# Feed-forward output products on the two 64-row halves of the array, in four phases of paired blocks

## The chip, the cores and the metric

The kernel runs on one core of a Trainium2 chip. The metric is the device time of one execution in microseconds. Three runs of the kernel before took 1286.21, 1286.5 and 1287.46 us (median 1286.5). A measurement of this kernel tells about 0.2% from no change.

In the profile, PE is the TensorE matrix engine and PEld its weight loads, DVE the vector engine, ACT the scalar engine, POOL the GpSimd engine, and SPq the queue that starts most transfers.

## What is computed

One inference step of a two-layer decoder trunk, for 512 prompt tokens and 8 x 8 sample tokens: layer 0 is a gated recurrent block, layer 1 sliding-window attention, and each is followed by a SwiGLU feed-forward block. All sizes are float32. The change touches the feed-forward block only:

```python
def swiglu(h, w_in, w_out):
    gate, up = jnp.split(h @ w_in, 2, axis=-1)
    return (jax.nn.silu(gate) * up) @ w_out
...
h = modulate(rms_norm(x, norm_g[l, 1]), sh2, sc2)
x = x + g2[:, None, :] * swiglu(h, ffn_w_in[l], ffn_w_out[l])
```

with D_MODEL = 1024 and D_FF = 2816, so `w_out` has 22 x 8 tiles of 128 x 128. The gain g2 (and the shifts and scales) come from modulation products, `silu(c) @ ada_w`, which the kernel spreads over its whole length.

## The kernel before

**Layout.** The 576 tokens are split into two halves h = 0, 1 of HC = 288 columns (256 prompt tokens and 32 sample tokens); features lie on the 128 partitions. The stream `x[h]` stays in SBUF as 8 chunks of 128 features.

**Products.** float32 products are made of single-pass ones (type fp32r): each operand is split into a rounded high part and the rest, and hi*hi + hi*lo + lo*hi are summed in one PSUM bank. So one 128 x 128 weight tile against 288 columns is three TensorE instructions (`product`), each of which loads its own weights. In the profile's names `wh` are split weights, `h`, `sl`, `ta`, `tb`, `td` split activations and working tiles, `mm` PSUM banks. There are 6 such banks (`ps()`), and 2 more for the modulation products (`ada`).

**Weights.** A weight unit is loaded into a `raw` buffer by a transfer, then converted: ACT copies the rounded high part into one `wh` slot, DVE subtracts it to make the low part in another (`convert`). There are 10 slots of 1024 columns (2 * NHI). A unit of feed-forward output weights holds all n middle tiles of a group for one output chunk m, n x 128 columns: 768 in groups of 6, 512 in the last group of 4. It is used for both token halves and then dropped (`drop`), which frees its slots. `todo` lists the conversions in order, and `pump` starts them as slots come free.

**The feed-forward block.** `ffn(l, ...)` goes through the 22 middle tiles in GROUPS = (6, 6, 6, 4). For each group, the input stage makes the group's middle tiles (silu(gate) * up), in seven products each by a scheme that saves one in eight (`seven`, operands "11", "22", "S1" to "S4", "12"); POOL, ACT and DVE prepare the operands, and `whole` splits each finished middle tile into two `sl` tiles, `mid[h][f]`. Then the output stage, `out(k, m, h)`, adds for each output chunk m and token half h the product of the group's n middle tiles into one bank: 3 n instructions, a *block*. `residual` (DVE, with a small sum on POOL) adds the gated block to the stream. A stage has 16 blocks, in the order (m = 0, h = 0), (0, 1), (1, 0), (1, 1), ...; in the last group h = 1 runs LEAD = 4 chunks behind h = 0, so that the norm of h = 0 can begin early. In layer 1's last group `final_chunk` transposes each finished chunk for the output. There are two layers of four groups, so eight output stages of 16 blocks.

**Order of the work.** Every instruction is recorded with its estimated cost and the operations it depends on (`Recorder.add`); `schedule` then simulates the engines and writes one fixed order for each of them, and TensorE's instructions may be interleaved one by one. `together()` records several instructions as one piece that isn't split: so far the batches of modulation products, which use the array as four strips of 32 columns, and the paired score products of the attention, which use 64 rows each. A cost table in `Engine.record` holds the estimates; `mode` names the array's form, and the simulation adds 100 ns where it changes.

Of the kernel before, what the change touches and what calls it, by code (L numbers as in the profile page):

```python
# [13 lines left out]
F32R = mybir.dt.float32r  # L14
# [5 lines left out]
P = 128  # L20
D = 1024
KC = D // P
# [5 lines left out]
HC = 288  # L28
# [100 lines left out]
class Recorder:  # L129
# [9 lines left out]
        self.batch = None  # L139

    @contextmanager
    def together(self):

        self.batch = []
        yield
        b, self.batch = self.batch, None

        def emit():
            for x in b:
                x[1]()  # L150

        self.add(b[0][0], emit, sum(x[2] for x in b), [y for x in b for y in x[3]], [y for x in b for y in x[4]], mode=self.mode)

    def tile(self, pool, kind, cap, reserve, shape, dt, name):
        sh = self.shadow[kind in ("mm", "ada")].tile(shape, dt, tag=name, bufs=1, name="shadow_" + name)
# [223 lines left out]
class Engine:  # L379
# [8 lines left out]
    def record(self, name, args, kw):  # L388
        eng, obj = self.eng, self.obj
        outs, ins, vals = [], [], list(args) + list(kw.values())  # L390
        isap = lambda v: hasattr(v, "ap") and hasattr(v, "tensor")
        first = kw["out"] if "out" in kw else args[0]
        outs.append(first)
        if isap(kw.get("accum_out")):
            outs.append(kw["accum_out"])
        ins = [v for v in vals if isap(v) and not any(v is o for o in outs)]
        f = max([_free(x) for x in outs + ins])
        scal = len([x for x in ins if x is not kw.get("accum_out") and _free(x) == 1 and len(x.ap) <= 2 and f > 1])
        ps_ = any(_is_psum(x) for x in ins)
        func, lat = None, 0  # L400

        reads = [x for x in (list(args) if "out" in kw else list(args[1:])) + [v for n, v in kw.items() if n not in ("out", "accum_out")] if isap(x)]
        wide = [x for x in reads if not _is_psum(x) and not str(x.space).endswith("DRAM") and (_free(x) > 1 or f == 1)]
        port = eng == "POOL" and name != "dma_start" and bool(wide) or eng == "DVE" and not ps_ and (len(wide) > 1 or name == "tensor_scalar" and f > 1)
        port = (2 if eng == "POOL" and f <= 40 else 1) if port else 0
        mode = 0
        if name == "matmul":
            if kw.get("start") is not True:
                ins.append(first)
            n = _free(first)  # L410
            dt = args[2].dtype
            cost = max(n + 32, 264) / 2.4 if dt == F32R else max(214.0 if first.ap[0][1] > 32 else 134.0, n * 4 / 2.4)
            if dt == F32 and 64 in (first.ap[0][1], args[1].ap[0][1]) and n >= P:

                mode = 1 if args[1].ap[0][1] == 64 else 2
                cost = n * 2 / 2.4 + 20
            if first.ap[0][1] == 32 and args[1].ap[0][1] == P and n >= P:
                cost = n / 2.4 + 30 if dt == F32 else n / 9.6 + 15
                mode = 3
        elif name == "transpose":  # L420
            cost = 107.0
        elif name == "dma_start":
            src = args[1]
            n = max(_free(first) * first.ap[0][1], _free(src) * src.ap[0][1])
            cost, lat = (460.0 if eng == "SP" else 1020.0), n * 4 / 335.0 + 5
        elif eng == "ACT":
            cost = (52 if ps_ else 94) + 0.8333 * f + (0, 90, 187)[min(scal, 2)] + (96 if isap(kw.get("accum_out")) else 0)
            func = str(args[2]).split(".")[-1] if name == "activation" else "Copy"
        elif eng == "DVE":
            if name == "reciprocal":  # L430
                cost = 62 + 6.28 * f
            elif name == "memset":
                cost = 20 + 0.5 * f
            elif name == "tensor_tensor_scan":
                cost = 70 + 2.1 * f
            else:
                cost = 67 + 1.0417 * f + (61 if scal and name == "scalar_tensor_tensor" else 0)
        else:
            if name == "tensor_tensor":
                cost = 150 + (165 if ALU.pow in vals else 2.4) * f  # L440
            elif name == "memset":
                cost = 35 + 0.83 * f
            elif name == "tensor_scalar":
                cost = 260 + 3.33 * f if scal else 95 + 1.05 * f
            else:
                cost = 120 + 3.3 * min(f, 32) + max(f - 32, 0) * 1.1
        self.rec.add(eng, lambda: getattr(obj, name)(*map(real, args), **{k: real(v) for k, v in kw.items()}), cost, outs, ins, func, lat, port, mode)  # L447


class Slots:  # L450
# [6 lines left out]
    def __call__(self, dt=None):  # L457
        self.live += 1
        self.n += 1
        self.peak = max(self.peak, self.live)  # L460
        return Slot(self, self.rec.tile(self.pool, self.kind, self.bufs, self.reserve, [P, self.w], dt or self.dt, f"{self.kind}{self.n}"))


class Slot:
# [9 lines left out]
def trunk_kernel(ctx, tc, a):  # L474
    nc = tc.nc
    rec = Recorder(a["shadow"])
# [6 lines left out]
    def const(shape, name, dt=F32):  # L483
        return cp.tile(shape, dt, tag=name, name=name)
# [3 lines left out]
    def ps(pool=pmm, tag="mm"):  # L488
        cnt[0] += 1
        return rec.tile(pool, tag, NMM if tag == "mm" else (8 - NMM), RMM if tag == "mm" else 1, [P, 512], F32, f"{tag}{cnt[0]}")  # L490
# [4 lines left out]
    x = [const([P, KC, HC], f"x{h}") for h in range(2)]  # L495
# [26 lines left out]
    nsp4 = const([P, KC], "nsp4")  # L522
    snk = const([P, 52], "snk")
    hgb = const([P, 16], "hgb")

    make_identity(nc, ident)
    nc.gpsimd.memset(ones, 1.0)
# [402 lines left out]
    class Unit:  # L930
        def __init__(self, kc, srcs):
            self.kc, self.srcs, self.raw, self.hi, self.lo = kc, srcs, None, None, None
            self.left = 2
# [14 lines left out]
    def convert():  # L948
        u = units[nconv[0]]
        if u.raw is None:  # L950
            load_more()
        n = u.kc * P
        u.hi, u.lo = whs(), whs()
        with early(EW):
            S.copy(u.hi.r[:, 0:n], u.raw.f[:, 0:n])
            V.tensor_tensor(u.lo.r[:, 0:n], u.raw.f[:, 0:n], u.hi.f[:, 0:n], ALU.subtract)
        u.raw.done()
        nconv[0] += 1
        nhi[0] += 1

    def drop(u):
        u.left -= 1
        if u.left == 0:
            u.hi.done()
            u.lo.done()
            nhi[0] -= 1

    def unit_cols(w, c0, k0=0, kc=KC):
# [200 lines left out]
    def ffn(l, g, after):  # L1169
# [80 lines left out]
        def queue():  # L1250
            for k, bs in enumerate(blocks):
                for i in range(max(PLAIN, sum(GROUPS[:k])), sum(GROUPS[: k + 1])):
                    st = steps(i)
                    if i == PLAIN:
                        nxt = steps(i + 1)
                        for s_, names in ((st, ("11", "12")), (nxt, ("11", "12")), (st, ("22", "S1", "S2", "S3", "S4")), (nxt, ("22", "S1", "S2", "S3", "S4"))):
                            for n in names:
                                todo.append((1, s_[n]))
                    elif i > PLAIN + 1:
                        for n in ("11", "22", "S1", "S2", "12", "S3", "S4"):  # L1260
                            todo.append((1, st[n]))
                for _ in outs[k][1]:
                    todo.append((2, convert))

        def pump(want=lambda: True):
            while todo and (whs.live + todo[0][0] <= 2 * NHI):
                todo.popleft()[1]()
            assert want()
            load_more()
# [66 lines left out]
            split(m[0].r[:, 0:HC], m[1].r[:, 0:HC], t.f[:, 0:HC])  # L1336
            t.done()

        def out(k, m, h):
            f0, us = outs[k]  # L1340
            n, u = GROUPS[k], us[m]
            pump(lambda: u.hi is not None)
            o = ps()
            product(o[:, 0:HC], u, [(mid[h][f][0].r[:, 0:HC], mid[h][f][1].r[:, 0:HC]) for f in range(f0, f0 + n)])
            last = k == len(GROUPS) - 1
            residual(h, o, m, g, last)
            if last and l == 1:
                final_chunk(h, m)
            drop(u)
            pump()  # L1350
            if m == KC - 1:
                for f in range(f0, f0 + n):
                    for s_ in mid[h][f]:
                        s_.done()
                if last:
                    after(h)

        def emit():
            if l == 1:
# [3 lines left out]
            for k in range(len(GROUPS)):  # L1363
# [23 lines left out]
                            for s_ in pq:  # L1387
                                s_.done()
                lead = LEAD if k == len(GROUPS) - 1 else 0
                for j in range(KC + lead):  # L1390
                    for h, m in ((0, j), (1, j - lead)):
                        if 0 <= m < KC:
                            out(k, m, h)
                            if h == 0:
                                ada_pace(1)
                if k < len(GROUPS) - 1:
                    seven(n_, "11")

# [590 lines left out]
```

## Time and profile before

| | |
|---|---|
| median of 3 runs | 1286.5 us (1286.21 to 1287.46) |
| span of the profiled execution | 1287.3 us |
| TensorE busy | 1250.5 us (97%) |
| DVE, ACT, POOL busy | 913.8, 659.3, 482.6 us |
| mean granted TensorE clock | 0.991 |
| bytes moved | 165.40 MB, mean 128 GB/s |

The profiled execution took 0.8 us more than the median. Rows by lines give the engine, the operation, out <- in, shapes, the count, then busy time and mean duration; rows of the timeline give start and length in us and how many instructions are merged; rows of the chain of waits give start and length of each piece of the chain that ended last; rows of windows give the length of the stretch, then for each engine busy time and count, the granted clock, the DMA share and GB/s. In "64*128 64x256" the array works with 64 rows and 128 columns, on 64 partitions and 256 moving columns. All recorded operations have one line, L447 before and L453 after the change, so they are told apart by tiles.

### The profile page before, as it was taken

The numbers are of one execution on the slowest core, as the hardware profiler recorded it, in microseconds if no ns is written. First come the engines' busy times: TensorE is split into PE (matmuls) and PEld (weight loads), VectorE is DVE, ScalarE is ACT, GpSimd is POOL, SyncE is SP. The second block draws the span as 40 slices with busy tenths as digits, with TensorE's granted clock in tenths as the row PEclk, the third lists the DMA queues.
The fourth block names the chain that finished last, engine by engine and source line by source line (L and its number), as shares of the span: only waits on it lengthen the run. The fifth ranks groups of instructions, "written<-read, shape, count | busy, mean of one in ns | idle before, by whom it ended". The sixth has DMA issues, their size and how long they took to land.

```text
span 1287.3 us, 25427 instructions
## 1 busy us (share of the span) xinstructions
PE 1250.5 (97%) x9532; PEld 1173.3 (91%) x9532; DVE 913.8 (71%) x2161; ACT 659.3 (51%) x1470; POOL 482.6 (37%) x710
## 2 busy tenths in 40 slices
PE   7999999999999999999989999999999999999997
PEld 5788899898999999999988987899999999999997
DVE  6988785886478457646679787448965875885777
ACT  4789873753245235414466678438533542552433
POOL 3476630142354145324234435110424533642422
PEclk9999999999999999999999999899999999999998
DMA  9956454525456655554342321233241332233232
GB/s 306 326 165 217 151 164 148 169 63 184 135 152 188 192 170 164 164 180 140 107 97 48 60 75 51 68 94 111 75 123 50 99 115 80 69 107 91 67 98 74
DMA packets 223982, 165.40 MB, mean 128 GB/s; under 512 B 23758, under 2 KB 209066, under 8 KB 223827
## 3 DMA queue, kind: packets, MB, share of 16 engines
q1 hardware_dynamic: 223410, 163.45, 42.2%
q8 instruction: 75, 1.23, 0.4%
q14 instruction: 49, 0.39, 0.1%
q0 software_dynamic: 448, 0.32, 0.1%
HBM read 160.85 MB, written 4.87 MB: 129 GB/s over the span
## 4 chain that ended last, share of the span: by engine, by line
PE 76%; DVE 12%; ACT 4%; POOL 3%; issue 2%; DMA 1%; SPq 1%; ACTq 0%; POOLq 0%; DVEq 0%
PE mm L447 72%; PE ada L447 4%; DVE sl L447 4%; DVE wh L447 3%; POOL raw L447 3%; ACT wh L447 1%; DVE ta L447 1%; DVE h L447 1%; DVE td L447 1%; DVE tb L447 1%; ACT ta L447 1%; ACT L447 1%; ACT h L447 1%; SPq L447 1%; DMA wh<-in_ada_w_dram 1%
## 5 line engine op out<-in xcount | busy, mean ns | idle before, releaser
L447 PE MATMUL mm<-h,wh 128*128 128x288 f32 x4128 | 598.7, 299 | 9.2 <-ACT h L447 4.2
L447 PEld LDWEIGHTS mm<-h,wh 128*128 128x128 f32 x4128 | 563.6, 189 | 30.2 <-issue 10.7
L447 PE MATMUL mm<-sl,wh 128*128 128x288 f32 x3218 | 460.5, 296 | 0.8 <-ACT ta L447 0.8
L447 PEld LDWEIGHTS mm<-sl,wh 128*128 128x128 f32 x3218 | 436.6, 188 | 8.6 <-issue 6.7
L447 ACT CAST wh<-raw 128x512 fp32r<-128x512 f32 (+2 forms) x388 | 266.8, 710 | 301.4 <-PE mm L447 221.0
L447 DVE TENSOR_TENSOR wh<-raw,wh 128x512 fp32r<-128x512 f32 (+2 forms) x388 | 358.3, 948 | 50.5 <-ACT wh L447 46.7
L447 DVE SCALAR_TENSOR_TENSOR x<-mm,mods,x 128x256 f32<-128x256 f32 x160 | 77.1, 482 | 153.1 <-PE mm L447 152.9
L447 POOL TENSOR_TENSOR raw<-raw 128x512 f32<-128x512 f32 x76 | 110.9, 1460 | 188.1 <-DVE wh L447 187.5
L447 POOL TENSOR_TENSOR x<-x,ta 128x32 f32<-128x32 f32 x152 | 54.0, 355 | 308.7 <-DVE ta L447 308.5
L447 POOL TENSOR_TENSOR raw<-raw,raw 128x512 f32<-128x512 f32 x76 | 112.8, 1486 | 3.7
L447 PE MATMUL mm<-tb,wh 128*128 128x288 f32 (+1 forms) x488 | 89.6, 299 | 7.9 <-DVE td L447 5.4
L447 PEld LDWEIGHTS mm<-tb,wh 128*128 128x128 f32 x488 | 72.2, 188 | 12.4 <-DVE td L447 8.8
L447 POOL TENSOR_TENSOR td<-td,td 128x288 f32<-128x288 f32 x38 | 31.1, 817 | 113.7 <-ACT td L447 105.1
L447 PE MATMUL mm<-ta,wh 128*128 128x288 f32 (+1 forms) x254 | 56.0, 298 | 0.0
L447 DVE TENSOR_TENSOR td<-mm,td 128x288 f32<-128x288 f32 x76 | 33.4, 452 | 26.8 <-PE mm L447 26.5
L447 ACT ACTIVATE ta<-x 128x288 f32<-128x288 f32 x56 | 24.8, 444 | 50.9 <-POOL x L447 48.0
L447 PE MATMUL ada<-reg,cz 128*32 128x512 f32 (+1 forms) x448 | 50.3, 553 | 0.4 <-DMA reg<-in_ada_w_dram 0.2
L447 DVE TENSOR_TENSOR sl<-ta,sl 128x288 fp32r<-128x288 f32 x54 | 45.7, 849 | 2.2 <-ACT sl L447 2.0
L447 ACT COPY td<-mm 128x256 f32<-128x256 f32 (+1 forms) x102 | 33.8, 353 | 23.9 <-PE mm L447 20.8
L447 ACT ACTIVATE ta<-mm 128x288 f32<-128x288 f32 x54 | 21.4, 411 | 45.4 <-PE mm L447 44.9
L447 PEld LDWEIGHTS mm<-ta,wh 128*128 128x128 f32 x254 | 41.6, 188 | 1.7 <-ACT wh L447 0.8
L447 ACT ACTIVATE ta<-ta,stat 128x256 f32<-128x256 f32 (+2 forms) x72 | 32.3, 471 | 17.8 <-DVE stat L447 17.0
(202 smaller groups left out, 1250.4 us busy)
## 6 DMA issues: line engine op xcount, KB each, us to landing
raw<-in_ffn_w_in_dram SPq DMA_DIRECT2D x88, 512.0 KB
reg<-in_ada_w_dram SPq DMA_DIRECT2D x80, 512.0 KB
raw<-in_ffn_w_out_dram SPq DMA_DIRECT2D x48, 384.0 KB
raw<-in_rnn_w_in_dram SPq DMA_DIRECT2D x16, 512.0 KB
reg<-in_kv_ada_w_dram SPq DMA_DIRECT2D x16, 512.0 KB
wh<-in_ada_w_dram SPq DMA_DIRECT2D x24, 256.0 KB
raw<-in_rnn_w_out_dram SPq DMA_DIRECT2D x8, 512.0 KB
raw<-in_ffn_w_out_dram SPq DMA_DIRECT2D x16, 256.0 KB
```

Source lines behind the costliest of these rows:

```text
L447: self.rec.add(eng, lambda: getattr(obj, name)(*map(real, args), **{k: real(v) for k, v in kw.items()}), cost, outs, ins, func, lat, port, ...
```

## The change

`out4` takes the place of `out`. It handles four blocks a, b, c, d of an output stage at once, in four banks, and splits each 128-row product into two products of 64 rows: the upper rows of weights and activations, and the lower ones. Two such products of different blocks form a pair that `together` keeps in one piece. There are four phases of 3 n pairs:

1. a on the upper half of the array, b on the lower;
2. c on the upper half, d on the lower;
3. b on the upper half, a on the lower;
4. d on the upper half, c on the lower.

After each of the first two phases ACT copies one element of each of the phase's two banks to `seen`. Since a bank that is read must not be written meanwhile, the third and fourth phase wait for these copies. `chain` makes every pair depend on the one before, in the order written. After phase 3, a and b go to `residual`, after phase 4, c and d. Four blocks need four units of weights at most, so units of 512 columns keep both parts in one slot (`Part`). The cost table gets an entry for fp32r products on 64 rows. The order of blocks, the groups and the arithmetic stay as they were.

```diff
@@ -139,7 +139,7 @@
-    def together(self):
+    def together(self, chain=None):
@@ -149,7 +149,10 @@
-        self.add(b[0][0], emit, sum(x[2] for x in b), [y for x in b for y in x[3]], [y for x in b for y in x[4]], mode=self.mode)
+        op = self.add(b[0][0], emit, sum(x[2] for x in b), [y for x in b for y in x[3]], [y for x in b for y in x[4]], mode=self.mode)
+        if chain is not None:
+            op.preds.update(chain)
+            chain[:] = [op]
@@ -414,6 +417,9 @@
+            if dt == F32R and args[1].ap[0][1] == 64:
+                mode = 1
+                cost = n / 4.8 + 1
@@ -461,6 +467,13 @@
+class Part:
+
+    def __init__(self, slot, o):
+        self.r, self.f, self.done = slot.r[:, o : o + 512], slot.f[:, o : o + 512], slot.done
@@ -522,6 +535,7 @@
+    seen = small[:, 1:2]
@@ -950,7 +964,11 @@
-        u.hi, u.lo = whs(), whs()
+        if n <= 512:
+            w = whs()
+            u.hi, u.lo = Part(w, 0), Part(w, 512)
+        else:
+            u.hi, u.lo = whs(), whs()
@@ -1336,24 +1355,49 @@
+        chain = []
+        ROWS = [slice(0, 64), slice(64, P)]
+
+        def parts(u, h, f0):
+
+            out = []
+            for k in range(u.kc):
+                xh, xl = [y.r[:, 0:HC] for y in mid[h][f0 + k]]
+                hi, lo = u.hi.r[:, k * P : (k + 1) * P], u.lo.r[:, k * P : (k + 1) * P]
+                out += [(hi, xh), (hi, xl), (lo, xh)]
+            return out
+
-        def out(k, m, h):
+        def out4(k, four):
+
             f0, us = outs[k]
-            n, u = GROUPS[k], us[m]
-            pump(lambda: u.hi is not None)
-            o = ps()
-            product(o[:, 0:HC], u, [(mid[h][f][0].r[:, 0:HC], mid[h][f][1].r[:, 0:HC]) for f in range(f0, f0 + n)])
+            n = GROUPS[k]
             last = k == len(GROUPS) - 1
-            residual(h, o, m, g, last)
...
+            pump(lambda: all(us[m].hi is not None for m, _ in four))
+            o = [ps()[:, 0:HC] for _ in four]
+            mms = [parts(us[m], h, f0) for m, h in four]
+            for q, pair in enumerate(((0, 1), (2, 3), (1, 0), (3, 2))):
+                for j in range(3 * n):
+                    with rec.together(chain):
+                        for i, r in zip(pair, ROWS):
+                            w, v = mms[i][j]
+                            T.matmul(o[i], w[r], v[r], start=q < 2 and j == 0, stop=j == 3 * n - 1, skip_group_check=True)
+                if q < 2:
+                    for i in pair:
+                        S.copy(seen[0:1], o[i][0:1, 0:1])
+                    continue
+                for i in sorted(pair):
+                    m, h = four[i]
+                    residual(h, o[i], m, g, last)
+                    if last and l == 1:
+                        final_chunk(h, m)
+                    drop(us[m])
+                    pump()
...
@@ -1387,12 +1431,10 @@
-                for j in range(KC + lead):
-                    for h, m in ((0, j), (1, j - lead)):
-                        if 0 <= m < KC:
-                            out(k, m, h)
-                            if h == 0:
-                                ada_pace(1)
+                blocks_ = [(m, h) for j in range(KC + lead) for h, m in ((0, j), (1, j - lead)) if 0 <= m < KC]
+                for j in range(0, 2 * KC, 4):
+                    out4(k, blocks_[j : j + 4])
+                    ada_pace(sum(h == 0 for _, h in blocks_[j : j + 4]))
```

How this moves instructions is seen at two places. The first is TensorE at the start of an output stage of layer 1 (the group of middle tiles 6 to 11), around the last middle tile's arrival. Before, with block mm471 (h = 0) and block mm472 (h = 1); `sl336` and `sl337` are the high and low part of the last middle tile for h = 0:

```order
L447 MATMUL mm471_13561<-sl332_13466,wh408_13419 128x288
L447 MATMUL mm471_13561<-sl336_13571,wh407_13406 128x288 [waits Activation_49]
L447 MATMUL mm472_13591<-sl314_12907,wh407_13406 128x288
L447 MATMUL mm472_13591<-sl315_12928,wh407_13406 128x288
L447 MATMUL mm472_13591<-sl314_12907,wh408_13419 128x288
L447 MATMUL mm471_13561<-sl337_13587,wh407_13406 128x288 [waits DVE_49]
L447 MATMUL mm471_13561<-sl336_13571,wh408_13419 128x288
L447 MATMUL mm472_13591<-sl318_13050,wh407_13406 128x288
```

After, at the end of the first phase of the same stage; `sl334` and `sl335` are the last middle tile for h = 1:

```order
L453 MATMUL mm471_14977<-sl332_14881,wh400_14834 128x288
L453 MATMUL mm472_14979<-sl330_14874,wh400_14834 128x288
L453 MATMUL mm471_14977<-sl336_14992,wh399_14821 128x288 [waits Activation_49]
L453 MATMUL mm472_14979<-sl334_15000,wh399_14821 128x288 [waits Activation_49]
L453 MATMUL mm471_14977<-sl337_15020,wh399_14821 128x288 [waits DVE_49]
L453 MATMUL mm472_14979<-sl335_15010,wh399_14821 128x288
L453 MATMUL mm471_14977<-sl336_14992,wh400_14834 128x288
L453 MATMUL mm472_14979<-sl334_15000,wh400_14834 128x288
L453 MATMUL mm473_15028<-sl316_14339,wh401_14852 128x288
```

Three products of the next block stood between the high part and the low part of the last tile; now the pairs follow in their own order, and both token halves' last tiles are wanted at the 16th of 18 pairs. The row behind the 18th pair is the first of the second phase.

The second place is ACT in the same output stage, from the last casts of the middle tile on. Before:

```order
L447 CAST sl336_13571<-ta412_13513 128x288 [waits DVE_49]
L447 CAST sl334_13575<-td147_13472 128x288 [waits Pool_49]
L447 CAST wh417_13618<-raw167_13481 128x768 [waits DMAHW2_49,PE_49,Activation_49]
L447 CAST wh419_13670<-raw168_13509 128x768 [waits DMAHW3_49,PE_49,Activation_49]
L447 CAST wh421_13722<-raw169_13549 128x768 [waits DMAHW4_49,PE_49,Activation_49]
```

After:

```order
L453 CAST sl336_14992<-ta412_14929 128x288 [waits DVE_49]
L453 CAST sl334_15000<-td147_14888 128x288 [waits Pool_49]
L453 COPY small_67<-mm471_14977 1x1 [waits PE_49]
L453 COPY small_67<-mm472_14979 1x1 [waits PE_49,Activation_49]
L453 COPY small_67<-mm473_15028 1x1 [waits PE_49,Activation_49]
L453 COPY small_67<-mm474_15030 1x1 [waits PE_49,Activation_49]
L453 CAST wh409_15110<-raw167_14894 128x768 [waits DMAHW2_49,PE_49]
L453 CAST wh411_15162<-raw168_14925 128x768 [waits DMAHW3_49,PE_49]
L453 COPY small_67<-mm475_15154 1x1 [waits PE_49,Activation_49]
```

Four one-element copies, each waiting for TensorE, now stand ahead of the casts of the weight units for later blocks, and again after every two of them.

More of the change, by code (lines that the diff above doesn't have):

```diff
@@ L964, in drop @@
             u.hi.done()
-            u.lo.done()
+            if u.kc * P > 512:
+                u.lo.done()
             nhi[0] -= 1
@@ L1261, in queue @@
                             todo.append((1, st[n]))
-                for _ in outs[k][1]:
-                    todo.append((2, convert))
+                for u in outs[k][1]:
+                    todo.append((2 if u.kc * P > 512 else 1, convert))
         def pump(want=lambda: True):
@@ L1337, in whole @@
             t.done()
-        def out(k, m, h):
+        chain = []
[8 more added lines that the diff above has]
+        def out4(k, four):
             f0, us = outs[k]
-            n, u = GROUPS[k], us[m]
-            pump(lambda: u.hi is not None)
-            o = ps()
-            product(o[:, 0:HC], u, [(mid[h][f][0].r[:, 0:HC], mid[h][f][1].r[:, 0:HC]) for f in range(f0, f0 + n)])
+            n = GROUPS[k]
             last = k == len(GROUPS) - 1
-            residual(h, o, m, g, last)
[L1347 to L1356, printed above, removed]
+            pump(lambda: all(us[m].hi is not None for m, _ in four))
[18 more added lines that the diff above has]
+                    pump()
+                    if m == KC - 1:
+                        for f in range(f0, f0 + n):
+                            for s_ in mid[h][f]:
+                                s_.done()
+                        if last:
+                            after(h)
         def emit():
```

## The prediction

> **What bounds the kernel now.** I read the page's first part, the chain of waits by line and in order of time, the windows, and then single stretches of the timeline.
>
> ```profile
> span 1287.3 us, 25427 instructions
> PE 1250.5 (97%) x9532; PEld 1173.3 (91%) x9532; DVE 913.8 (71%) x2161; ACT 659.3 (51%) x1470; POOL 482.6 (37%) x710
> PE 76%; DVE 12%; ACT 4%; POOL 3%; issue 2%; DMA 1%; SPq 1%; ACTq 0%; POOLq 0%; DVEq 0%
> ...
> 1045.97 58.41 PE mm L447 x439
> 1104.39 1.37 DVE wh L447 x2
> ...
> 1150.10 0.84 ACT wh L447
> 1151.00 0.84 issue
> 1152.34 83.03 PE mm L447 x623
> ```
>
> TensorE is busy for 97% of the span. The chain runs through it alone wherever output products are made (the pieces of 58.41 and 83.03 us); between them, in layer 1, it passes through DVE, POOL and ACT, which prepare weight operands. So a shorter output stage shortens the program one for one, as long as what follows it was waiting for TensorE.
>
> ```profile
> L447 PE MATMUL mm<-sl,wh 128*128 128x288 f32 x282 | 37.5, 295 | 0.0
> ...
> 1000.00:1046.00 46.00, 45.55 (x339) 44.66 (x337) 40.06 (x56) 25.56 (x52) 26.81 (x20) 1.00 0.30 83
> ...
> 951.00:988.00 37.00, 37.00 (x282) 37.00 (x281) 19.88 (x46) 7.62 (x13) 10.73 (x18) 1.00 0.29 87
> ```
>
> The first row is one output stage (951 to 988 us) by lines: 282 products in 37.5 us, the last lasting 0.295, so one starts every (37.5 - 0.295) / 281 = 132.4 ns, with no idle time and (last row) a granted clock of 1.00. DVE is busy for only 19.88 of 37.00 us there, ACT for 7.62. In the weight-bound stretch from 1000 to 1046 us DVE has 40.06 of 46.
>
> **The change part by part.** Per layer there are 22 x 8 x 2 x 3 = 1056 output products, 2112 in all. Each becomes two products of 64 rows, and two of these, for different blocks and banks, run as a pair. So 2112 products of 132.4 ns become 2112 pairs, and all hangs on the price of a pair. No single-pass product on half the array is in this trace. The nearest rows are the score products of the attention, 64 rows in pairs, in float32, which makes two records of one product (four products, eight records):
>
> ```profile
> 779.65 1.14 PE L447 MATMUL mm<-wh,sl 64*128 64x256 f32 x8
> ...
> 779.65 0.19 PEld L447 LDWEIGHTS mm<-wh,sl 64*128 64x128 f32 x2 [0.23 <-issue]
> ...
> 779.76 0.41 PEld L447 LDWEIGHTS mm<-wh,sl 64*128 64x128 f32 x4
> ...
> 779.97 0.41 PEld L447 LDWEIGHTS mm<-wh,sl 64*128 64x128 f32 x4
> ...
> 780.19 0.19 PEld L447 LDWEIGHTS mm<-wh,sl 64*128 64x128 f32 x1
> ```
>
> Two weight loads go out together, and the next two follow 0.21 to 0.22 us later (779.76, 779.97, 780.19): eight records fit in 1.14 us. So the halves do run at the same time, weights and products both, at 215 ns for a pair of records of 256 columns, 0.84 ns per column. The whole-array product takes 132.4 / 288 = 0.46 ns per column, a little over half of that. From this come three prices of a new pair:
> - floor: both halves stream at 0.42 ns per column, half of the float32 row: 288 x 0.42 = 121 ns;
> - near end: each half keeps the whole-array interval: 132.4 ns;
> - far end: the float32 pair delivers 2 x 256 columns in 215 ns; if 0.42 ns per column is the limit of both halves together, 576 columns take 242 ns.
>
> I take 122 ns, the floor and 1 ns, since the paired row, nearest in form, shows no start-up beyond its columns. That saves 2112 x (132.4 - 122) = **22.0 us**. At the near end it saves nothing; at the far end it costs 2112 x 109.6 = 231 us. Each half needs its own 128-column weight load within the 122 ns:
>
> ```profile
> 781.89 0.27 PE L447 MATMUL mm<-ident,tb 128*128 128x128 f32 x1
> 782.00 0.27 PE L447 MATMUL mm<-ident,ta 128*128 128x128 f32 x1
> 782.11 0.27 PE L447 MATMUL mm<-ident,tb 128*128 128x128 f32 x1
> ...
> L447 PE MATMUL ada<-wh,cz 128*32 128x128 f32 x58 | 2.5, 279 | 0.0
> L447 PE MATMUL mm<-h,wh 128*128 128x288 f32 x7 | 1.7, 340 | 0.0
> ```
>
> Transposes, each with its own 128-column load, start 0.11 us apart, so a load fits, with some 10 ns to spare. Issue fits too: in the 3.6 us from 25.7 us on (the last two rows) 65 products start, each with its load, 55 ns apart, where a pair needs 61.
>
> [...]
>
> *Changes of array form.* In the order of the two programs the array's form (rows by columns in use) changes 255 times instead of 238, mostly where a weight-bound stage and an output stage meet (the pairs stand in 14 stretches). The price:
>
> ```profile
> 446.76 0.42 PE L447 MATMUL mm<-sl,wh 128*128 128x288 f32 x2
> 447.11 0.64 PE L447 MATMUL ada<-reg,cz 128*32 128x512 f32 x4
> ...
> 448.97 0.40 PE L447 MATMUL mm<-sl,wh 128*128 128x288 f32 x1
> ```
>
> The last whole-array product starts at 446.76 + 0.13 = 446.89, the next form at 447.11, 0.22 us later instead of 0.13, and it then waits for a weight load that nothing hides (on the way back the first product lasts 0.40 instead of 0.295 us, 0.105 more). 0.09 and 0.105 make about 0.2 us each, so 17 x 0.2 = **+3.4 us**.
>
> *Starts of the eight output stages.* The first pairs read both halves of the stream, and the last of the group's middle tiles at pair 16 of 18; the strict order of pairs leaves nothing to fill with.
>
> ```profile
> 950.41 0.30 PE L447 MATMUL mm<-ta,wh 128*128 128x288 f32 x1
> 950.55 3.71 PE L447 MATMUL mm<-sl,wh 128*128 128x288 f32 x27
> ...
> 951.53 0.46 DVE L447 TENSOR_TENSOR ta<-ta,mm 128x288 f32<-128x288 f32 x1
> 951.90 0.95 DVE L447 TENSOR_TENSOR wh<-raw,wh 128x768 fp32r<-128x768 f32 x1
> 952.77 0.45 DVE L447 TENSOR_TENSOR sl<-ta,sl 128x288 fp32r<-128x288 f32 x1
> ```
>
> The last low part (sl) is done at 953.22, 2.67 us after the first product at 950.55; before, three products of the next block filled in. The pairs want it after 16 x 0.122 = 1.95 us: up to 0.7 us late, and the signal's way on top. Where a batch of modulation products stands in between (1.85 us, first row of the next fence), it covers this; in layer 1 nothing does. I take 0.5 us at each of eight, **+4 us** (bounds 0 and 8).
>
> *The reads.*
>
> ```profile
> 447.18 1.85 PE ada L447 x16
> ...
> L447 ACT COPY td<-mm 128x32 f32<-128x32 f32 x16 | 3.1, 197 | 0.0
> ```
>
> ACT gets 128 one-element copies, 0.2 us each by its smallest PSUM copies (second row); they lie in its idle time (7.62 of 37 busy). What queues behind them are casts that wait for weight slots anyway. Each pair of reads has a whole phase to arrive, 18 x 122 ns = 2.2 us, or 1.46 us in the last groups, against an estimated 0.8 us (0.16 for the last product to drain, 0.2 for the copy, as much for each of two signals): 0. If that cover fails, 64 phase ends wait at most 0.8 us, 51 us.
>
> *The end.* The last phase finishes two blocks instead of one; one residual, one norm sum and one block's gain come later:
>
> ```profile
> 1277.73 0.48 DVE L447 SCALAR_TENSOR_TENSOR x<-mm,mods,x 128x256 f32<-128x256 f32 x1
> 1278.13 0.18 DVE L447 TENSOR_TENSOR ta<-mm,mods 128x32 f32<-128x32 f32 x1
> ...
> 1278.71 0.45 DVE L447 TENSOR_TENSOR acc<-acc,ta 128x288 f32<-128x288 f32 x1
> ```
>
> 0.48 + 0.18 + 0.45 and a little, **+1.3 us**. Half-width weight slots in the last groups and earlier conversion of two units change what is ready when, not how much is done: 0.
>
> Sum: 1287.3 - 22.0 + 3.4 + 4.0 + 1.3 = 1274.0 us against the profiled execution, which is 0.8 above the median of the runs (1286.5): **1273 us**.
>
> **The rivals.**
> 1. *The halves run together but keep the 132.4 ns, so only the joints are left: slower.* For it: the 11 ns over the floor appear in all single-pass products, and no row says that the array's form causes them; if they belong to the fast stream, each half has them. Against: the float32 pair has none. 1287.3 + 3.4 + 4.0 + 1.3 - 0.8 = 1295. It decides as soon as a pair costs over 132.4 - 8.7 / 2.112 = 128.3 ns.
> 2. *The halves share one stream and do not overlap at this rate*, so the change does not do what it says: 242 ns per pair, 1273 + 2112 x 0.120 = about 1526. For it: the paired row is at exactly the rate where this limit would not show. Against: nothing else, only that weight loads of both halves were seen side by side.
> 3. *Pairs cost 122, but the weight-bound stretches of layer 1 become longer.* DVE has 6 us free in 46 there; a four holds two units (four slots) to its third phase, where a block held one, so fewer operands are ready ahead. 27 operands took 46 us, 1.7 us each; one operand late at each of six borders is 10 us: 1283. Against: the chain enters TensorE again with hardly a gap.
>
> **How the numbers follow.** Forecast 0.48, rival 1 0.29, rival 2 0.11, rival 3 0.08, a pair price in between (about 128 ns, within 0.2%) 0.04. A measurement of this kernel tells 0.2% (2.6 us) from no change, so faster means below 1283.9. Faster: 0.48 and half of rival 3, 0.52; same: 0.04 and the other half, 0.08; slower: 0.29 + 0.11 = 0.40. The likeliest case's own range is 1265 (no cost at starts, floor price) to 1281. The range for 8 in 10 takes in rival 1: 1263 to 1297.
>
> **What would show it.** Right: a window inside an output stage has the second record of a pair within 10 ns of the first, and about 61 ns per 64-row product, so 576 of them in 35 us, with no TensorE idle at the phase ends and a granted clock of 1.00. Rival 1: about 66 ns per 64-row product. Rival 2: about 121. Rival 3: DVE or POOL as releaser of TensorE after the output stages of layer 1. The joints show as TensorE waits on ACT or DVE for sl at the first pairs, about 0.5 us each. The prediction is wrong if a pair costs over 128 ns, or if the reads hold TensorE at phase ends.

## The result, and the profile after

The changed kernel takes 1308.86 us (median of 4 runs, 1305.83 to 1310.77) against 1286.89 us for the kernel before in the same comparison: ratio 1.0167, 95% interval 1.0152 to 1.0181. It is 22 us slower; 1273 was forecast, with a range of 1263 to 1297.

The first lines of its page, then the output stage from 1068 to 1105 us (layer 1, group 1), by lines and as a window:

```profile
span 1309.0 us, 29864 instructions
PE 1263.1 (96%) x11644; PEld 1182.0 (90%) x11644; DVE 893.7 (68%) x2161; ACT 677.6 (52%) x1598; POOL 489.8 (37%) x710
...
L453 PE MATMUL mm<-sl,wh 64*128 64x288 f32 x564 | 37.6, 292 | 0.0
...
1068.00:1105.00 37.00, 37.00 (x564) 36.88 (x562) 15.85 (x42) 10.21 (x29) 12.22 (x19) 1.00 0.28 82
```

564 half products are 282 pairs, in 37.6 us with no idle time and the full clock: (37.6 - 0.292) / 563 x 2 = 132.5 ns per pair, where a whole-array product took 132.4. To 0.1 ns a pair costs what it replaces. That explains a gain of nothing; the 22 us come from other places. I compared the two traces by the time of the same residual and input products. Of the 21.7 us between the two spans, 2.3 are there 55 us after the start, long before the change; 4 arise where layer 0 ends (about 665 to 685 us), 3 at the first output stage of layer 1, under 1 at each of the others, and some 10 from the last output stage to the end.

The first output stage of layer 1, in the changed kernel, by the timeline of TensorE (start, length, what, count, and in brackets the idle time before and its releaser):

```profile
955.00 2.25 PE L453 MATMUL mm<-sl,wh 64*128 64x288 f32 x30
957.18 1.05 PE L453 MATMUL mm<-tb,wh 128*128 128x288 f32 x6
958.07 0.97 PE L453 MATMUL mm<-sl,wh 128*128 128x288 f32 x6
959.59 0.67 PE L453 MATMUL mm<-tb,wh 128*128 128x288 f32 x3 [0.55 <-DVE td L453]
...
962.46 0.40 PE L453 MATMUL mm<-sl,wh 64*128 64x288 f32 x2 [1.01 <-ACT sl L453]
963.24 3.04 PE L453 MATMUL mm<-sl,wh 64*128 64x288 f32 x42 [0.37 <-DVE sl L453]
```

Fifteen pairs run, then whole-array products for the last middle tile, then the 16th pair waits 1.01 us for that tile's high part and the 17th 0.37 for its low part. In the kernel before nothing is waited for at this place: single output products fill in, three here, then products of the input stage, then twelve products that are in part output products again:

```profile
946.95 0.56 PE L447 MATMUL mm<-sl,wh 128*128 128x288 f32 x3
947.34 0.96 PE L447 MATMUL mm<-tb,wh 128*128 128x288 f32 x6
948.13 1.77 PE L447 MATMUL mm<-sl,wh 128*128 128x288 f32 x12
```

The end of layer 1, after, by the same timeline and by windows (length, then PE, PEld, DVE, ACT, POOL busy and count, granted clock, DMA share, GB/s):

```profile
1274.88 6.61 PE L453 MATMUL mm<-sl,wh 64*128 64x288 f32 x95 [0.20 <-DVE h L453]
1281.42 1.27 PE L453 MATMUL mm<-ident,x 128*32 128x128 f32 x10
...
1285.07 1.67 PE L453 MATMUL mm<-ident,x 128*128 128x128 f32 x6 [1.13 <-DVE x L453]
1286.53 1.05 PE L453 MATMUL mm<-small,ta 128*128 128x1 f32 x6
1287.51 8.78 PE L453 MATMUL mm<-sl,wh 64*128 64x288 f32 x96
...
1281.00:1288.00 7.00, 5.30 (x39) 4.37 (x37) 5.97 (x29) 1.72 (x4) 0.97 (x3) 0.82 0.02 4
1288.00:1296.00 8.00, 8.00 (x96) 8.00 (x94) 2.86 (x9) 2.78 (x8) 1.50 (x5) 0.73 0.42 148
```

Between the last two sets of four blocks TensorE does 6 us of transposes, norm sums and waiting; then 48 pairs take 8.78 us instead of 6.4, because the granted clock is down (0.82 and 0.73 in these windows). The clock's record has it at one half from 1285.5 to 1292.3 us.

### The profile page after: what moved, and what is told of

It is laid out like the page before. It is cut to its first block, busy times and chain, and to the rows that moved or that the text cites. A ratio compares the mean times of both kernels' runs of the same rounds, so it can differ in the third digit from the quotient of the medians.

```text
span 1309.0 us, 29864 instructions
## 1 busy us (share of the span) xinstructions
PE 1263.1 (96%) x11644; PEld 1182.0 (90%) x11644; DVE 893.7 (68%) x2161; ACT 677.6 (52%) x1598; POOL 489.8 (37%) x710
## 4 chain that ended last, share of the span: by engine, by line
PE 76%; DVE 12%; ACT 5%; POOL 2%; issue 2%; DMA 1%; SPq 1%; ACTq 0%; POOLq 0%; DVEq 0%
PE mm L453 72%; PE ada L453 4%; DVE wh L453 4%; DVE sl L453 3%; POOL raw L453 1%; DVE ta L453 1%; DVE h L453 1%; ACT wh L453 1%; ACT h L453 1%; ACT tb L453 1%; ACT ta L453 1%; DVE td L453 1%; DVE tb L453 1%; ACT L453 1%; DMA reg<-in_ada_w_dram 1%
## 5 line engine op out<-in xcount | busy, mean ns | idle before, releaser
L453 PE MATMUL mm<-sl,wh 64*128 64x288 f32 (+1 forms) x5330 | 460.7, 294 | 2.8 <-ACT sl L453 1.2
L453 PEld LDWEIGHTS mm<-sl,wh 64*128 64x128 f32 (+1 forms) x5330 | 438.4, 186 | 12.4 <-issue 6.9
L453 DVE TENSOR_TENSOR wh<-raw,wh 128x512 fp32r<-128x512 f32 (+2 forms) x388 | 344.6, 916 | 54.9 <-ACT wh L453 52.1
L453 POOL TENSOR_TENSOR x<-x,ta 128x32 f32<-128x32 f32 x152 | 63.8, 420 | 324.6 <-DVE ta L453 324.6
L453 POOL TENSOR_TENSOR raw<-raw 128x512 f32<-128x512 f32 x76 | 108.1, 1423 | 182.4 <-DVE wh L453 178.8
L453 ACT COPY small<-mm 1x1 f32<-1x1 f32 x128 | 18.9, 148 | 106.0 <-PE mm L453 104.0
L453 ACT ACTIVATE ta<-mm 128x288 f32<-128x288 f32 x54 | 21.4, 411 | 42.9 <-PE mm L453 42.6
```

## The experiments

All ratios are to the kernel before, measured on the same chip beside them; times are medians.

**The halves, or the four blocks?** Phases, chain, banks and reads stay; each phase runs whole-array products that alternate between its two blocks.

```diff
-                for j in range(3 * n):
+                for j in range(0, 3 * n, 2):
                     with rec.together(chain):
-                        for i, r in zip(pair, ROWS):
-                            w, v = mms[i][j]
-                            T.matmul(o[i], w[r], v[r], ...)
+                        for i in pair:
+                            w, v = mms[i][j // 2 + (q // 2) * (3 * n // 2)]
+                            T.matmul(o[i], w, v, ...)
```

> The same four blocks, phases, chain and one-element reads, but each phase runs 18 (or 12) whole-array products alternating between its two blocks instead of pairs of 64-row products; the sums are the same. Theory (a pair costs what one whole-array product costs, 132 ns; the loss comes from taking four blocks at once): about 1305 us, only the 17 extra changes of array form (3.4 us) and some luck gone. Rival (the halves themselves are the loss, a pair costs more than the trace of the changed kernel makes it look): about 1290 us.

1293.93 us, ratio 1.0049 (1.0032 to 1.0067). My theory fell. The four-block order is nearly harmless; using half of the array in it costs 1.2% more. Yet it isn't the pair's price, which is 132.5 ns in the trace. One thing besides the halves is different here: a block's products with the later middle tiles come in the third and fourth phase only, so the wait for the last tile at the first output stage of layer 1 is gone. By the traces against the kernel before that stage loses 3.2 us in the changed kernel and 0.2 here, so some 3 of the 15 us between the two belong to the order of the products. In this kernel's timeline at the end of layer 1 (first rows of several such groups) transposes stand between products, a few at a time:

```profile
1255.62 0.38 PE L453 MATMUL mm<-ident,x 128*128 128x128 f32 x2
1255.76 0.52 PE L453 MATMUL mm<-sl,wh 128*128 128x288 f32 x2
1256.11 0.49 PE L453 MATMUL mm<-ident,x 128*32 128x128 f32 x3
1256.36 0.51 PE L453 MATMUL mm<-sl,wh 128*128 128x288 f32 x2
```

With pairs they are collected into blocks of 6 to 20, since `schedule` adds a cost for each change of the array's form; what they wait for stands open.

**The last stage of each layer block by block**, the other six in pairs:

```diff
+                if k == len(GROUPS) - 1:
+                    for m, h in blocks_:
+                        out(k, m, h)
...
+                    continue
                 for j in range(0, 2 * KC, 4):
                     out4(k, blocks_[j : j + 4])
```

> The last output stage of both layers (groups of 4 middle tiles) block by block as in the kernel before, the other six stages in pairs. Theory (the loss sits where a layer ends: four banks at once, the norm and the final transposes behind them, and a halved clock after the idle time): 1309 - 11.7 (end) - 4.0 (end of layer 0) = about 1293 us. Rival (the loss is spread over all stages): 1309 x one quarter less of 22, about 1303 us.

1295.64 us, ratio 1.0056 (1.0041 to 1.0071): by the ratios 14 of the 22 us sit in the two last stages. That is the first theory's case, though the time is 2.6 us above the one that it gave.

**Only the very last stage block by block** (the same with `l == 1 and` in the condition).

> The changed kernel with only the very last output stage (layer 1, group of 4) block by block. Theory (the end of layer 1 costs about 10 of the 22 us, by the trace): 1309 - 10 = 1299 us, and the 4 us at the end of layer 0 remain. Rival (the two ends share the 13 us that both gave together evenly): about 1302 us.

1300.70 us, ratio 1.0096 (1.0080 to 1.0113). Between the two numbers that I had set, and nearer to neither by much: by the ratios the end of layer 1 costs 0.0167 - 0.0096, 9.1 us, the end of layer 0 0.0096 - 0.0056, 5.1 us, each by about 3 us uncertain. The traces agree at the end of layer 1: from the last product of its input stage to the end of the program they have 42.9 us in the kernel before, 52.9 in the changed kernel and 43.3 here.

**More banks at the end.** The final transposes go to the two banks of the modulation products:

```diff
-        t = aux()
+        t = ps(pada, "ada")
```

> The changed kernel, but the final transposes of layer 1 use the two PSUM banks of the modulation products, which are done by then, instead of the six banks that the blocks need. Theory (at the end the fours starve for banks): the last group loses most of its waits, 1309 - 7 = about 1302 us. Rival (the end is late because two blocks finish at once and the order of pairs is strict): within 2 us of the changed kernel, about 1308 us.

1304.08 us, ratio 1.0124 (1.0107 to 1.0141), 5.5 us better by the ratios: between theory and rival. In the trace the stretch from the last input product to the end takes 48.3 us instead of 52.9, against 42.9 before. Bank shortage is part of the cost at the end, not all of it. The same line in the kernel before:

> The kernel before, whole blocks, with the final transposes of layer 1 in the two PSUM banks of the modulation products. Theory (one block at a time never starves for banks): within 1.5 us of before, 1287. Rival (banks are short at the end in any case, and the changed kernel only shows it more): 2 to 5 us faster than before.

1287.45 us, ratio 0.9992 (0.9978 to 1.0006): nothing. One block at a time is not short of banks, so the shortage is of the change's making.

**The planner's cost** of a half product, in the table that `schedule` goes by:

```diff
-                cost = n / 4.8 + 1
+                cost = (n + 32) / 4.8
```

> The changed kernel with the planner's cost of a 64-row product set to (288 + 32) / 4.8 = 66.7 ns, which the trace shows, instead of 61. Theory (the planner's estimate matters little): within 3 us of 1309. Rival (the orders of DVE and ACT, planned for a faster TensorE, cause the waits at layer 1's start and the ends): 1295 to 1300 us.

1308.74 us, ratio 1.0160 (1.0145 to 1.0176): no difference to the changed kernel. The wrong estimate was not the reason.

**The planner not told of the form** (`mode = 1` left out for half products).

> The changed kernel, with the planner not told that a pair is another form of the array, so it may put transposes and whole-array products between pairs; the forms change 286 times instead of 255. Theory (pairs cannot be filled in without a change of form, 0.2 us each, whichever way it is planned): what is won in waits at the ends is paid in changes, 1309 - 10 + 6 = about 1305 us, between 1300 and 1312. Rival (only the planner's caution makes the ends slow): under 1298 us.

1303.01 us, ratio 1.0101 (1.0079 to 1.0124). It lies in the theory's range: 31 more changes of form, and still 8.5 us better by the ratios, but far from the 1298 that would have put everything on the planner's caution. The two traces show where it gains. By input products that the kernel before runs at 623, 757 and 842 us it is 1.1, 5.4 and 7.8 us ahead of the changed kernel. The first step is the end of layer 0: norm sums and transposes now stand between the pairs, and TensorE waits 1.9 us for ACT's `h` there instead of 6.4. In the second the clock is at one half for 3.4 us instead of 10.2. At the end of layer 1 it gains nothing: 53.2 us from the last input product to the end, against 52.9. There transposes stand between the pairs, and the waits that this saves are paid in changes of form (first rows of several such groups):

```profile
1256.80 0.44 PE L452 MATMUL mm<-ident,x 128*128 128x128 f32 x2
1257.16 0.53 PE L452 MATMUL mm<-sl,wh 64*128 64x288 f32 x4
1257.62 0.50 PE L452 MATMUL mm<-ident,x 128*32 128x128 f32 x3
1258.06 0.54 PE L452 MATMUL mm<-sl,wh 64*128 64x288 f32 x4
```

Over the 21 places of this kind in that stretch, the first transpose starts 0.22 us after the last half product (0.13 after a whole-array product in the kernel before), and the first half product 0.20 us after the last transpose (0.03 before): by these medians 0.27 us more each time, 5.6 us in all.

**The price of a pair, by width and type.** Two kernels, one with whole-array products and one with pairs, both with other moving operands in the same five stages, whose sums are therefore not those of the task. At 400 and 512 columns half of the columns are read twice; as bf16 only the upper two bytes of each element are read.

```diff
+            kind = {(0, 1): "wide", (0, 2): "bf16", (1, 0): 192, (1, 1): 256, (1, 2): 400}.get((l, k))
+            if kind == "bf16":
+                return o[:, 0:HC], w.bitcast(BF16)[:, 1::2], v.bitcast(BF16)[:, 1::2]
...
+                v2 = v[:, 0 : c // 2].unsqueeze(1).to_broadcast([r, 2, c // 2])
...
+                return o[:, 0:kind], w, v[:, 0:kind]
```

> The kernel before with other moving operands in five of its output stages (layer, group): (0, 1) 512 columns, the first 256 of the tile read twice; (0, 2) 288 columns, both operands read as bf16, the upper two bytes of each element; (1, 0) 192 columns, (1, 1) 256 columns in all products of a block but its first; (1, 2) 400 columns, 200 read twice. The rest is as before, so sums of these stages are not the reference's. Read from the trace: ns from one product to the next. If each 4-byte column costs 0.46 ns: 235, -, 110 (weight load), 118, 184. If an instruction costs 0.417 ns a column and 12 ns: 226, -, 110, 119, 179. If the weight load makes the 132 ns: 192 and 256 columns also 132, 400 and 512 at 167 and 213. bf16: 122 if four-byte elements cause the 11 ns, 132 otherwise.

> The same five moving operands in the changed kernel, with the last output stage of each layer as before (its whole-array products serve as a check). Read from the trace: ns from one pair to the next. Theory (each half has the price of a whole-array product, whatever makes it up): the same numbers as in the whole-array kernel within 2 ns at every width and for bf16. Rival (both halves together meet a limit of their own, such as one stream or one bank write per column, that happens to give 132 at 288 columns): other numbers, for bf16 above all, or 512 columns over 240.

By lines, inside each stage; first whole-array products at 400 and 512 columns and bf16:

```profile
L447 PE MATMUL mm<-sl,wh 128*128 128x400 f32 x284 | 52.1, 345 | 0.0
...
L447 PE MATMUL mm<-sl,wh 128*128 128x512 f32 x157 | 36.5, 393 | 0.0
...
L447 PE MATMUL mm<-sl,wh 128*128 128x288 bf16 x155 | 20.0, 289 | 0.0
```

then half products:

```profile
L453 PE MATMUL mm<-sl,wh 64*128 64x400 f32 x562 | 51.4, 341 | 0.0
...
L453 PE MATMUL mm<-sl,wh 64*128 64x512 f32 x212 | 24.7, 390 | 0.0
...
L453 PE MATMUL mm<-sl,wh 64*128 64x288 bf16 x332 | 21.4, 286 | 0.0
```

Busy time less the last duration, over the count less one, gives the price; for pairs it is doubled. At 192 and 256 columns, where the first product of a block keeps its 288, half the median distance of every second whole-array product, and the median distance of every second half product, stand in its place:

| columns | whole-array product, ns | pair, ns |
|---|---|---|
| 192 | 112 | 112 |
| 256 | 118.5 | 118 |
| 288 | 132.4 | 132.5 |
| 400 | 182.9 | 182.0 |
| 512 | 231.5 | 230.4 |
| 288, bf16 | 128.0 | 127.6 |

Within 1.1 ns the same at every width and for either type: each half has the price of a whole-array product of its own, as the theory said. What makes up the price is less tidy than any of the three guesses: about 0.44 ns per column and 6 ns, over a floor of 112 at 192 columns, and bf16 takes only 4.4 ns off. None of the start-up of an instruction, the weight load and the four bytes makes up the 11 ns alone; what does stays open, but it is paid whichever part of the array runs the product.

**Pairs in the two middle stages of layer 1 only, and in its first only** (the condition for block by block is `l == 0 or k not in (1, 2)`, and `l == 0 or k > 0`).

> Pairs only in the two middle stages of layer 1 (groups 1 and 2), all others block by block; the half-width slots of the last group stay. Theory (a pair costs what a whole-array product costs): only two entries and exits, 4 changes of form more than before, 0.2 us each, and up to 1 us at each start: 0.3 to 2 us over the kernel before, 1288 to 1291. Had a pair cost 122 ns, 576 pairs would have saved 6 us: about 1282.

1291.62 us, ratio 1.0034 (1.0023 to 1.0046), above what I expected. The trace puts 0.8 us of it into the two stages, the rest elsewhere, above all before and at the end of layer 0, where this kernel has no pairs.

> Pairs only in the first output stage of layer 1, all others block by block. By the trace of the changed kernel this stage loses 3.2 us, to waits for the last middle tiles and a stretch of whole-array products between its first pairs: 2.5 to 4 us over the kernel before, about 1292. Rival (the 3.2 us belong to an accident of the order that the planner makes of all stages together): within 1.5 us of before.

1293.85 us, ratio 1.0047 (1.0034 to 1.0060). In the trace this stage loses 3.4 us, as expected; by the ratio the kernel loses 6.1, so again there seems to be something besides.

**Only the half-width slots of the change.** What both had in common, without any pairs.

> No pairs at all: all eight output stages block by block, and of the change only the half-width weight slots of the last groups are left. In the trace of the kernel with pairs in the two middle stages alone, only 0.8 us of its 4 us arise in those stages. Theory (the slots change which conversions run ahead at the end of layer 0, and cost 2 to 3 us by themselves): 1289 to 1290 us. Rival (the slots are free; what is left there is run-to-run clock and order): within 1 us of the kernel before, about 1287.

1292.30 us, ratio 1.0035 (1.0021 to 1.0048): 4.5 us from the one part that I had called free, more than the theory's 2 to 3. Windows around the end of layer 0, first of the kernel before, then with the slots alone, then of the changed kernel:

```profile
660.00:667.00 7.00, 5.64 (x37) 4.64 (x35) 5.76 (x23) 7.00 (x17) 3.19 (x5) 1.00 0.19 39
667.00:678.00 11.00, 8.93 (x63) 8.37 (x64) 8.45 (x20) 8.08 (x18) 5.55 (x7) 1.00 0.52 98
```

```profile
660.00:667.00 7.00, 4.81 (x30) 3.84 (x28) 7.00 (x25) 6.09 (x16) 1.30 (x3) 1.00 0.00 1
667.00:678.00 11.00, 10.17 (x41) 9.06 (x42) 5.24 (x10) 5.37 (x13) 7.08 (x6) 0.53 0.51 96
```

```profile
664.00:671.00 7.00, 3.21 (x39) 2.67 (x35) 6.49 (x17) 3.10 (x7) 4.61 (x6) 1.00 0.37 77
671.00:678.00 7.00, 5.30 (x23) 5.30 (x23) 6.71 (x24) 6.95 (x18) 0.14 (x1) 0.51 0.37 75
```

TensorE is busy for 5.64 of 7 us before, for 4.81 with the slots, for 3.21 with the whole change; and in the two latter the granted clock then falls to a half, for 10.2 and 6.8 us by its record. The other traces bear this out: all eleven with the half-width slots have such a stretch of 6.8 or 10.2 us at the end of layer 0, and the three without them (the kernel before, the same with more banks, and the whole-array kernel of the widths) have none there. In the 11 us from 667 TensorE is busy for longer with the slots (10.17 against 8.93), but for 41 instructions instead of 63. Over the runs of this kernel time goes with the mean granted clock: 1287.14 us at 0.993, 1296.76 at 0.983. The kernel before, at 0.991 in most runs, varied from 1284.87 to 1290.30 in the same comparison.

**The account**, from ratios whose intervals are about 0.0015 to either side, so 2 us for one and about 3 for a difference of two:

| part | from | us |
|---|---|---|
| half-width slots | slots alone, 1.0035 | 4.5 |
| pairs in the six earlier stages | 1.0056 - 1.0035 | 2.7 |
| pairs at the end of layer 0 | 1.0096 - 1.0056 | 5.1 |
| pairs at the end of layer 1 | 1.0167 - 1.0096 | 9.1 |

## Why the prediction was wrong

*The price of a pair: the step that failed.* "I take 122 ns, the floor and 1 ns, since the paired row, nearest in form, shows no start-up beyond its columns." Measured: 132.5, so the saving of 22.0 us is nil. The row was near in form (two halves) but far in rate: float32 passes each column in 0.84 ns, and at twice that rate the product has a cost of its own, which the whole-array rows already showed and which I left out. They were the nearer row. The Trainium skill says in "TensorE: Matmul & The Clock Gate", section "Why this matters for your kernels", that a single product with 32 rows takes as long as one with 128, and that the gain of packing is concurrency. The trace agrees for 64 rows, to 0.1 ns a pair, and where all 128 rows were full before there was nothing left to gain. The first rival had this price. The second (no overlap) is excluded by the same row.

*Changes of form and starts: 3.4 and 4.0 us forecast.* The six earlier stages cost 2.7 us for both, by about 3 uncertain. In the program with only these in pairs there are 11 more changes than before, 2.2 us at 0.2 each. The wait at the first pairs is there as described (1.01 and 0.37 us on ACT and DVE for `sl`) in layer 1's first stage; at the other stages TensorE waits for `sl` only once more, 0.20 us at 436 us. Right in kind, and by the middle of that interval too high in size.

*The reads: 0.* Nothing in the waits of TensorE names them, and with them the whole-array phases are within 0.14% of the slots alone (1.0049 and 1.0035, inside the intervals). They were not tried by themselves.

*The end: 1.3 us forecast, 14.2 measured at both.* This is why even the first rival's 1295 was short. I counted one more residual; what counts is that four blocks hold four of six banks, that transposes and norm sums between pairs cost a change of form, so that they were put behind the pairs, and that the idle time halves the clock for the work behind it. More banks show the first at the end of layer 1 (5.5 us by the ratios, 4.6 in the trace). The planner not told of forms shows the second: at the end of layer 0 it gains 4.3 us in the trace, while at the end of layer 1 it only turns waits into changes. The two weren't tried together. In the whole-array phases, where transposes stand between products without that price, the stretch to the end of layer 1 takes 45.4 us instead of 52.9. The clock's part at the end of layer 1 is read from one trace: 8.78 - 6.4, 2.4 us.

*The slots: 0 forecast, 4.5 measured.* "Half-width weight slots ... change what is ready when, not how much is done: 0." The first half is true and the conclusion wrong: what was ready when moved the gaps at the end of layer 0 closer together, and the clock fell in every trace with these slots. In the one trace of the slots alone the program loses 3.6 us there (from 623 to 701 us) and has 1.6 of them back at 842 us, so how the 4.5 us of the runs are made up is not shown in full. Which conversion came too late was not settled either.

*The third rival* (longer weight-bound stretches in layer 1) did not happen: between the later output stages the two kernels stay within half a microsecond.

No version here beats the kernel before.

## What to carry to other kernels

Splitting a product that fills all rows into two half-array products gained nothing here: each half cost what the whole did, at every width tried. Before the price of an operation is taken from a neighbour in the trace, the neighbour must match in rate as well as in form; a row of the same rate and another form was the better guide. And a change that only moves work about, near a place where TensorE already has gaps, can cost several microseconds through the granted clock.

## What the runs showed of the hardware

The granted clock halves after idle time that is spread as well as after one long gap. With the slots alone the longest gap before the fall at 667 us was 1.37 us, and TensorE was busy for 4.81 of the 7 us. In the changed kernel one gap was 4.07 us:

```profile
668.03 0.60 PE L453 MATMUL mm<-ident,tst 128*128 128x128 f32 x3 [1.42 <-POOL tst L453]
672.70 5.17 PE L453 MATMUL mm<-h,wh 128*128 128x288 f32 x20 [4.07 <-ACT h L453]
```

The Trainium skill ("TensorE: Matmul & The Clock Gate", section "What's actually happening") has a free-running window of about 3.4 us of activity for this. The traces agree in so far as the half-clock stretches that end within the program last 3.4, 6.8, 10.2 or 13.7 us; gaps of at most 1.4 us before one of them show that a single long gap isn't needed.

The product at full rate costs about 0.44 ns a column and 6 ns from 256 to 512 columns, and 4.4 ns less at 288 columns when its operands are read as bf16. A switch between half products and transposes delayed the next instruction by 0.09 us one way and 0.18 the other, against whole-array products (medians of 21 places).
